# A chunked state recurrence: two heads in 64x64 products, or side by side in 128x128 products with block-diagonal operands

## The chip, the core and the metric

The kernel runs on one core of a Trainium2 chip, as one program. The metric is the device time of one execution in microseconds (us), the median of three runs. The engines are named as in the profile: PE is the matrix engine (TensorE; PEld is its weight load), DVE the vector engine, ACT the scalar engine, POOL GpSimd, and SP the engine that issues the DMAs.

## What is computed

One layer of a streaming encoder for 64 frames of a running stream and 512 of a new one (576 rows, width 1024): a norm, a combined projection, RWKV-7 time mixing, a gated mixer, a merge, a feed-forward part. The change is in time mixing. Each of 16 heads has a state S of 64x64 that goes from frame to frame:

```
def step(S, inp):
    r_t, w_t, k_t, v_t, a_t, b_t = inp
    sa = jnp.einsum('bhvk,bhk->bhv', S, a_t)
    S = S * w_t[:, :, None, :] + sa[..., None] * b_t[:, :, None, :] + v_t[..., None] * k_t[:, :, None, :]
    y = jnp.einsum('bhvk,bhk->bhv', S, r_t)
    return S, y
```

After it y is normalised by head, a bonus is added, and the sum is multiplied by a gate.

## The kernel before

The recurrence is not run frame by frame. The 576 frames are nine chunks of 64, the first of them the running stream's. In a chunk the removals (the a and b terms) depend on each other through a triangular 64x64 system, which is inverted; then the chunk needs only products with the state at its start. Heads go in eight pairs, head 0 of a pair on partitions 0 to 63 and head 1 on 64 to 127. The order is written for a pair as four generators, and each runs beside the generators of the neighbouring pairs.

- *Elements* (`elementwise`, lines 592 to 737): DVE, ACT and POOL make the rows AR, BK, AK and their factors from the projections r, k, v (tiles `pj`). PE makes the products `am` of one chunk's rows; DVE and POOL scale them into AB, AK and BK (lines 655 to 686). PE transposes BK (`tb`) and v (`tv`); ACT copies the results to BKt and Vt. The norms `n2` come from PE, `rn` is their reciprocal.
- *Inverse* (from line 739): AB goes out by DMA (`d_inv`) and comes back as M in 32x32 blocks. DVE runs 62 dependent operations in turns on Xt and X (lines 754 and 757). X goes out and back by DMA, DVE transposes (`T`, line 769), PE makes the two 32x32 products `mp` and `mu`, and ACT copies them to PT and AB.
- *Chain* (from line 793, printed below): nine chunks in eight steps, the first of which takes the running stream's chunk and the new one's first together. In a step the values product AK·Vt and the state product AR·S are summed in `pw`; ACT copies W; AB·W goes to `pz` and BKt·Vt to `pn`; ACT scales Z from `pz`; BKt·Z is added in `pn`; DVE makes the next S (line 825). Each product is two of 64x64, one head in the upper left and one in the lower right quarter of PE's array. `pw`, `pz` and `pn` are parts of one PSUM buffer `pc`, of which there is one. At the end of a pair the output rows `py` come from AR·S, AK·Vt and AB·Z over all chunks.
- *Finish* (from line 844): normalisation by DVE, ACT and POOL, nine transposes `to`, gate products `g`.

PE's order is written by `Weave`, a planner that keeps a clock of its own: a step that yields `LAT["W"]` is taken up again when its count of PE time has passed that latency, and between them it puts projection work three passes at a time (`pj`, later `gv`, each 128x128, in fp32r, as high and low parts in three products). The other engines are put in order by a scheduler, and each works strictly in its order; SP's DMA queue as well. ACT and POOL split the projection weights into `whi` and `wlo` in the same queues.

fp32 products take two passes of the array. Where the text below says a pair product, it means the two 64x64 products of two heads.

Of the kernel before, what the change touches and what calls it, by code (L numbers as in the profile page):

```python
# [12 lines left out]
P = 128  # L13
# [3 lines left out]
T = TS + TP  # L17
# [205 lines left out]
def layer(tc, I, O):  # L223
# [16 lines left out]
    cst = cp.tile([P, NCST], F32, name="cst")  # L240
# [4 lines left out]
    x0 = cst[0:3 * NU, C_X0:C_X0 + 11 * 32]  # L245
# [15 lines left out]
    def mmul(out, lhsT, rhs, **kw):  # L261
        n = 1
        for d in rhs.shape[1:]:
            n *= d
        clk.now += n * (1 if rhs.dtype == F32R else 4) / 2400
        return pe.matmul(out, lhsT, rhs, **kw)  # L266
# [205 lines left out]
    sp.dma_start(cst, I["cst"][:, 0:NCST])  # L472
# [18 lines left out]
    pool.memset(rmask[:, :, 0:1], 0.0)  # L491
    shc = cp.tile([P, 26, 2], F32, name="shc")
    s0 = cp.tile([P, NPAIR, HD], F32, name="s0")
    sp.dma_start(s0, I["s0"])
# [73 lines left out]
    rmul = ep.tile([P, NCH, P], F32, name="rmul")  # L568
    pool.tensor_copy(rmul[:, :, 64:P], mask[:, 64:P].unsqueeze(1).broadcast_to([P, NCH, 64]))
# [22 lines left out]
    def elementwise(E):  # L592
# [38 lines left out]
        s = ps1("n2")  # L631
        for c in range(NCH):
            p0 = 64 * (c % 2)
            mmul(s[p0:p0 + 64, c - c % 2:c - c % 2 + 2], q2[:, c * 64:(c + 1) * 64], bones[:, 0:P:64], start=True, stop=True)
        clk.now += LAT["n2t"]
        rn = rp.tile([P, NCH], F32, tag="rn", bufs=2, name="rn")
        for h in range(2):
            for par in range(2):
                dve.tensor_scalar(rn[64 * h:64 * h + 64, par::2], s[64 * par:64 * par + 64, h:10 - 2 * par:2], 1e-24, None, ALU.max)
        dve.reciprocal(rn, rn)  # L640
        pool.tensor_tensor(rmul[:, :, 0:64], mask[:, 0:64].unsqueeze(1).broadcast_to([P, NCH, 64]), rn.unsqueeze(2).broadcast_to([P, NCH, 64]), ALU.mult)
# [62 lines left out]
        Vt = rp.tile([P, NCH, HD], F32, tag="Vt", bufs=2, name="Vt")  # L704
        Z = rp.tile([P, NCH, HD], F32, tag="Z", bufs=2, name="Z")
        S = rp.tile([P, NCH + 2, HD], F32, tag="S", bufs=2, name="S")

        pvs = [ps1("tv").rearrange("p (j h v) -> p j h v", h=2, v=HD) for _ in range(2)]
        for j in range(5):
            t0 = min(j * P, T - P)  # L710
            mtrans(pvs[j // 4][:, j % 4].rearrange("p h v -> p (h v)"), v[:, t0:t0 + P], ident)
        for h, rows in enumerate(HR):
            for par in range(2):
                act.activation(Vt[rows, par:8:2, :], pvs[0][HR[par], :, h, :], ACT.Copy)
            act.activation(Vt[rows, 8, :], pvs[1][HR[1], 0, h, :], ACT.Copy)
        yield LAT["tv"]
        act.activation(S[:, 0, :], s0[:, hp_, :], ACT.Copy)
        pool.memset(S[:, 1, :], 0.0)
# [16 lines left out]
        E.update(AR=AR, AB=AB, AK=AK, BKt=BKt, Vt=Vt, Z=Z, S=S, eC=eC, rn=rn, bonus=bonus)  # L735
# [3 lines left out]
    def inverse(E):  # L739
        AB, di = E["AB"], d_inv[E["hp"]]  # L740
# [5 lines left out]
        X = rp.tile([n, 11, 32], F32, tag="X", name="X")  # L746
        pool.tensor_copy(X, x0.rearrange("p (i t) -> p i t", t=32))
# [10 lines left out]
        for g in range(3):  # L758
            r = (32 - g + 2) // 3
            sp.dma_start(di[1].rearrange("h c b s t -> (h c b) s t")[:, g:32:3, :], X[g * NU:(g + 1) * NU, 0:r, :])  # L760
        for h in range(2):
            for b in range(2):
                r0_ = 64 * h + 32 * b
                sp.dma_start(AB[r0_:r0_ + 32, :, 32 * b:32 * b + 32], di[1, h, :, b].rearrange("c s t -> s c t"))
        yield lat("U", E["hp"])
        T1 = rp.tile([P, NCH, 32], F32, tag="T1", name="T1")
        PT = rp.tile([P, NCH, 32], F32, tag="PT", name="PT")
        for h in range(2):
            dve.transpose(T1[64 * h:64 * h + 32], AB[64 * h:64 * h + 32, :, 0:32])
        yield lat("mp", E["hp"])  # L770
        pp = ps1("mp")
        for c in range(NCH):
            for h in range(2):
                a0, a1 = 64 * h, 64 * h + 32
                mmul(pp[a1:a1 + 32, c * 32:c * 32 + 32], AB[a0:a1, c, 32:64], T1[a0:a1, c, :], start=True, stop=True)
        for h in range(2):
            a1 = 64 * h + 32
            src = pp[a1:a1 + 32, 0:NCH * 32].rearrange("p (c t) -> p c t", t=32)
            act.activation(PT[a1:a1 + 32], src, ACT.Copy)
        yield lat("mu", E["hp"])  # L780
        pp = ps1("mu")
        for c in range(NCH):
            for h in range(2):
                a0, a1 = 64 * h, 64 * h + 32
                mmul(pp[a0:a1, c * 32:c * 32 + 32], PT[a1:a1 + 32, c, :], AB[a1:a1 + 32, c, 32:64], start=True, stop=True)
        for h in range(2):
            a0 = 64 * h
            src = pp[a0:a0 + 32, 0:NCH * 32].rearrange("p (c t) -> p c t", t=32)
            act.activation(AB[a0:a0 + 32, :, 32:64], src, ACT.Copy)
# [3 lines left out]
    def chain(E):  # L793
        AR, AB, AK, BKt, Vt, Z, S, eC, rn, hp_ = (E[n] for n in ("AR", "AB", "AK", "BKt", "Vt", "Z", "S", "eC", "rn", "hp"))
        Y = rp2.tile([P, NCH, HD], F32, tag="Y", bufs=2, name="Y")


        for cs in [(0, 1)] + [(c,) for c in range(2, NCH)]:
            n = len(cs)
            pw, pz, pn = ps1c("pc")[:, 0:384].rearrange("p (a i v) -> a p i v", a=3, v=64)  # L800
            first = lambda i: dict(start=i == 0, skip_group_check=True)
            for i, c in enumerate(cs):
                for rows in HR:
                    mmul(pw[rows, i], AK[rows, c, 0:64], Vt[rows, c, :], stop=False, **first(i))
            for i, c in enumerate(cs):
                for rows in HR:
                    mmul(pw[rows, i], AR[rows, c, 0:64], S[rows, c, :], start=False, stop=True, skip_group_check=True)
            W = rp.tile([P, 2, HD], F32, tag="W", bufs=2, name="W")
            act.activation(W[:, 0:n], pw[:, 0:n], ACT.Copy)  # L809
            yield LAT["W"]  # L810
            for i, c in enumerate(cs):
                for rows in HR:
                    mmul(pz[rows, i], AB[rows, c, 0:64], W[rows, i, :], stop=True, **first(i))
            for i, c in enumerate(cs):
                for rows in HR:
                    mmul(pn[rows, i], BKt[rows, c, 64:128], Vt[rows, c, :], start=False, stop=False, skip_group_check=True)
            for i, c in enumerate(cs):
                act.activation(Z[:, c, :], pz[:, i], ACT.Copy, scale=rn[:, c:c + 1])  # L818
            yield LAT["Z"]
            for i, c in enumerate(cs):  # L820
                for rows in HR:
                    mmul(pn[rows, i], BKt[rows, c, 0:64], Z[rows, c, :], start=False, stop=True, skip_group_check=True)
            for i, c in enumerate(cs):
                nxt = {0: NCH, NCH - 1: NCH + 1}.get(c, c + 1)
                dve.scalar_tensor_tensor(S[:, nxt, :], S[:, c, :], eC[:, c:c + 1], pn[:, i], ALU.mult, ALU.add)  # L825
                if nxt >= NCH:
                    sp.dma_start((O["wkv_s"] if c == 0 else O["wkv_p"])[hp_], S[:, nxt, :])
            if c < NCH - 1:
                yield LAT["S"]

        for c0, c1 in CV:
            py = ps1("py").rearrange("p (c t) -> p c t", t=64)
            for n, (w, w0, x) in enumerate(((AR, 64, S), (AK, 64, Vt), (AB, 64, Z))):
                for c in range(c0, c1):
                    for rows in HR:
                        mmul(py[rows, c - c0, :], w[rows, c, w0:w0 + 64], x[rows, c, :],
                             start=n == 0 and c == c0, stop=n == 2 and c == c1 - 1, skip_group_check=True)
            act.activation(Y[:, c0:c1, :], py[:, 0:c1 - c0], ACT.Copy)
            yield LAT["y"]
# [500 lines left out]
```

## Time and profile before

| | |
|---|---|
| median of 3 runs | 1281.55 us (1281.29 to 1284.96) |
| the profiled execution's own time | 1281.43 us |
| its span | 1279.6 us |
| granted clock of PE | 0.975 |
| time mixing in the profile | about 55 to 665 us, the next stage's products (`pb`) from 730 us |

In a row of the timeline stand the start in us, the duration (of all instructions of the row), the engine, the line, the operation, the tile written and the tiles read, the size of the array used, the shape, the count, and in brackets an idle time before it with what ended it. Matmuls overlap, so the price of one is the distance between the starts of neighbours, not its duration. A row of the waits gives who waited for whom, in all, how often and the longest. A row of the groups has the mean of one instruction in ns behind the busy time.

### The profile page before, as it was taken

Reading aid. Unit: us, or ns where it says so; the run is one execution under the profiler, and the core shown is the slowest. Engines: PE = TensorE matmul, PEld = TensorE weight load, DVE = VectorE, ACT = ScalarE, POOL = GpSimd, SP = SyncE. Lnnn points to the kernel's source line nnn. Section 1 sums busy time; section 2 is a strip of 40 time slices with the busy share of each in tenths; the row PEclk is TensorE's granted clock in tenths of the full one; section 3 lists DMA queues with packets and bytes.
Section 4 is the critical chain, followed back from the end, with each engine's and each line's share of the span. In section 5 each row is a group of like instructions: output and inputs, shape, how many; then the busy total and the mean of one; then the engine's idle time right before and its main releaser. Section 6 shows DMA issues by size and latency. Waiting matters only on the chain.

```text
span 1279.6 us, 26938 instructions
## 1 busy us (share of the span) xinstructions
PE 1209.6 (95%) x11306; PEld 1149.0 (90%) x11306; DVE 605.9 (47%) x1241; ACT 497.0 (39%) x976; POOL 615.6 (48%) x504
## 2 busy tenths in 40 slices
PE   7798999899989999999989999989999999999997
PEld 6798788889888988879889999989999999999997
DVE  5958656746575747464183533374333333310013
ACT  5644454545362645443351233453222222222220
POOL 6655243433534342442375645356655556544442
PEclk9899999899999999999999999989999999999998
DMA  5232222222221222323156543222222222242222
GB/s 194 72 103 85 69 80 71 87 60 89 69 94 58 78 84 75 88 81 105 52 180 198 157 151 109 84 108 82 83 83 83 84 85 85 83 160 79 87 74 75
DMA packets 72665, 122.35 MB, mean 96 GB/s; under 512 B 36032, under 2 KB 39360, under 8 KB 72544
## 3 DMA queue, kind: packets, MB, share of 16 engines
q1 hardware_dynamic: 72400, 120.56, 29.7%
q8 instruction: 89, 1.46, 0.5%
q14 instruction: 32, 0.26, 0.1%
q10 hardware_dynamic: 144, 0.07, 0.0%
HBM read 103.28 MB, written 17.33 MB: 94 GB/s over the span
## 4 chain that ended last, share of the span: by engine, by line
PE 72%; DVE 14%; DMA 4%; ACT 3%; issue 3%; POOL 2%; SPq 1%; DVEq 0%; ACTq 0%; POOLq 0%
PE fg L266 20%; PE po L266 14%; PE pj L266 13%; PE pb L266 4%; PE gv L266 4%; PE pc L266 4%; PE pa L266 3%; DVE Xt L754 3%; DVE X L757 3%; DMA M<-d_inv 2%; PE fp L266 1%; PE am L266 1%; PE z L266 1%; PE py L266 1%; POOL wlo L285 1%
## 5 line engine op out<-in xcount | busy, mean ns | idle before, releaser
L285 POOL TENSOR_TENSOR wlo<-raw,whi 128x512 fp32r<-128x512 f32 (+1 forms) x288 | 405.0, 1429 | 362.3 <-ACT whi L282 349.0
L282 ACT ACTIVATE whi<-raw 128x1024 fp32r<-128x1024 f32 x144 | 150.0, 1046 | 280.5 <-PE fg L266 172.5
L754 DVE TENSOR_TENSOR Xt<-X,M 108x84 f32<-108x84 f32 (+23 forms) x248 | 70.4, 284 | 34.2 <-DMA M<-d_inv 27.3
L757 DVE TENSOR_TENSOR X<-X,Xt 108x84 f32<-108x84 f32 (+23 forms) x248 | 70.6, 285 | 7.7
L1091 DVE TENSOR_TENSOR rs<-rs,nsq 128x288 f32<-128x288 f32 (+2 forms) x12 | 9.1, 756 | 105.5 <-ACT nsq L1090 105.5
L825 DVE SCALAR_TENSOR_TENSOR S<-S,eC,pc 128x64 f32<-128x64 f32 x72 | 19.3, 277 | 69.3 <-PE pc L266 61.5
L1159 DVE TENSOR_TENSOR ft<-ft,fg 128x288 f32<-128x288 f32 x40 | 16.4, 451 | 67.1 <-PE fg L266 65.5
L1153 DVE TENSOR_TENSOR fg<-fg,rs 128x288 f32<-128x288 f32 x40 | 16.5, 453 | 62.1 <-PE fg L266 62.0
L809 ACT ACTIVATE W<-pc 128x64 f32<-128x64 f32 (+1 forms) x64 | 14.7, 230 | 75.2 <-PE pc L266 74.6
L818 ACT ACTIVATE Z<-pc,rn 128x64 f32<-128x64 f32 x72 | 21.6, 312 | 46.8 <-PE pc L266 46.4
L1156 DVE SCALAR_TENSOR_TENSOR ft<-ft,fg 128x576 f32<-128x576 f32 (+1 forms) x24 | 28.6, 1192 | 19.0 <-ACT ft L1155 19.0
L627 POOL TENSOR_TENSOR aq<-aq,k 128x576 f32<-128x576 f32 x8 | 11.3, 1418 | 53.1 <-DVE k L458 51.8
L1157 POOL TENSOR_TENSOR ft<-ft,rs 128x576 f32<-128x576 f32 (+1 forms) x24 | 31.7, 1322 | 7.7 <-DVE ft L1156 7.7
L695 ACT ACTIVATE BKt<-tb 64x256 f32<-64x256 f32 (+1 forms) x96 | 31.2, 325 | 6.8 <-PE tb L270 5.3
L266 PE MATMUL pj<-h4l,whi 128*128 128x288 f32 x92 | 28.3, 308 | 5.5 <-DVE h4l L335 5.5
L266 PEld LDWEIGHTS pc<-Vt,AK 64*64 64x64 f32 x288 | 14.2, 137 | 21.2 <-DVE S L825 12.1
L266 PE MATMUL pc<-Vt,AK 64*64 64x64 f32 x288 | 22.6, 245 | 10.8 <-DVE S L825 10.6
L856 POOL TENSOR_TENSOR gm<-gm,mhalf 128x9 f32<-128x9 f32 x8 | 15.5, 1940 | 34.8 <-DVE gm L855 34.8
L266 PE MATMUL pj<-h5h,whi 128*128 128x288 f32 x92 | 31.1, 338 | 0.0
L266 PE MATMUL pj<-h4h,whi 128*128 128x288 f32 x92 | 30.9, 336 | 0.0
L266 PE MATMUL pj<-h3h,whi 128*128 128x288 f32 x92 | 30.5, 331 | 0.0
L266 PE MATMUL pj<-h6h,whi 128*128 128x288 f32 x92 | 29.8, 324 | 0.0
(1206 smaller groups left out, 4293.7 us busy)
## 6 DMA issues: line engine op xcount, KB each, us to landing
raw<-in_w_in SPq DMA_DIRECT2D x50, 512.0 KB
raw<-in_w_gate SPq DMA_DIRECT2D x22, 512.0 KB
raw<-in_w_up SPq DMA_DIRECT2D x22, 512.0 KB
raw<-in_w_down SPq DMA_DIRECT2D x16, 512.0 KB
raw<-in_w_gv SPq DMA_DIRECT2D x8, 512.0 KB
raw<-in_w_proj_a SPq DMA_DIRECT2D x8, 512.0 KB
raw<-in_w_proj_b SPq DMA_DIRECT2D x8, 512.0 KB
raw<-in_w_o SPq DMA_DIRECT2D x8, 512.0 KB
```

What stands on the lines that cost most here:

```text
L266: return pe.matmul(out, lhsT, rhs, **kw)
L282: keep(act.activation(hi[:, :cols], raw[:, :cols], ACT.Copy))
L285: keep(pool.tensor_tensor(lo[:, c0:c1], raw[:, c0:c1], f(hi[:, c0:c1]), ALU.subtract))
L695: act.activation(BKt[rows, c0:c1, part], pt[part, 0:c1 - c0, rows], ACT.Copy)
L754: ins = dve.tensor_tensor(t3, X[:, 0:r, s:s + 1].broadcast_to([n, r, w]), M[:, s:s + 1, s + 1:32].broadcast_to([n, r, w]), ALU.mult)
L757: dve.tensor_tensor(X[:, 0:r, s + 1:32], X[:, 0:r, s + 1:32], t3, ALU.add)
L818: act.activation(Z[:, c, :], pz[:, i], ACT.Copy, scale=rn[:, c:c + 1])
L825: dve.scalar_tensor_tensor(S[:, nxt, :], S[:, c, :], eC[:, c:c + 1], pn[:, i], ALU.mult, ALU.add)
L1153: keep(dve.tensor_tensor(g[:, HS[h]], pg, rs2[:, HS[h]], ALU.mult))
L1156: keep(dve.scalar_tensor_tensor(t[:, ts], t[:, ts], 1.0, g[:, ts], ALU.add, ALU.mult))
L1157: pool.tensor_tensor(t[:, ts], t[:, ts], rs2[:, ts], ALU.mult)
L1159: dve.tensor_tensor(t[:, HS[h]], t[:, HS[h]], pu, ALU.mult)
```

## The change

The chain's products use the full array. AK, AR, AB and BKt of two heads stand side by side as they are (64 rows that feed W and 64 that give output rows), and the moving side becomes block-diagonal: `VB` (values), `Sin` and `Sb` (state), `Wb` (W) have one head on rows and columns 0 to 63 and the other on 64 to 127, with zeros elsewhere that POOL writes once at the start. `ZV` holds Z of both heads above the values. A chunk has four products where there were five pair products: values AK·VB, state AR·Sb, removals AB·Wb, update BKt·ZV. The output rows come out of the first three on partitions 64 to 127, and the loop for `py` goes. For this the removal rows are multiplied out ahead (`g2`, 9 pair products a pair), `mu` has twice the products, and POOL subtracts the unit matrix (`eye`). ACT copies half of W and DVE the other; DVE makes ZV, ACT copies the output rows Y; S is updated by two DVE operations. Transposes `to` are five, not nine; the copies of `tb` and `tv` are fewer; VB and Sin are filled by DMAs, and X by a DMA instead of a POOL copy. In the planner, "y" goes from `LAT`, "S" is 1.1 instead of 0.945, "g2" is 1.5, and a full-array fp32 product counts as at least 128 columns wide.

```diff
-    "M": 5.011, "U": 27.0, "mp": 1.34, "mu": 1.593, "ch0": 1.796, "ch1": 21.42, "W": 0.789, "Z": 0.945, "y": 0.8, "S": 0.945, "gn1": 2.973, "gn2": 3.703, "to": 2.623, "to1": 0.41, "g": 1.513,
+    "M": 5.011, "U": 27.0, "mp": 1.34, "mu": 1.593, "ch0": 1.796, "ch1": 21.42, "W": 0.789, "Z": 0.945, "S": 1.1, "g2": 1.5, "gn1": 2.973, "gn2": 3.703, "to": 2.623, "to1": 0.41, "g": 1.513,
...
+    NWB = 2
+    fixed = lambda name, *shape: rp.tile([P, *shape], F32, name=name)
+    Sin = [fixed(f"Sin{i}", P) for i in range(2)]
+    Sb = [fixed(f"Sb{i}", P) for i in range(2)]
+    Wb = [fixed(f"Wb{i}", P) for i in range(NWB)]
+    VB = [fixed(f"VB{i}", NCH, P) for i in range(2)]
+    IV = fixed("IV", NCH, 64)
+    IT = fixed("IT", NCH, 64)
+    for t in (*VB, IV, *Sin, *Sb, *Wb):
+        pool.memset(t, 0.0)
...
-            for part in HR:
-                for rows in HR:
-                    act.activation(BKt[rows, c0:c1, part], pt[part, 0:c1 - c0, rows], ACT.Copy)
+            act.activation(BKt[:, c0:c1, :], pt[:, 0:c1 - c0], ACT.Copy)
...
+        for rows in HR:
+            sp.dma_start(vb[rows, :, rows], ZV[64:128, :, rows])
+            sp.dma_start(Sin[hp_ % 2][rows, rows], I["s0"][rows, hp_, :])
...
+        dve.transpose(IT.rearrange("p c t -> p (c t)"), IV.rearrange("p c t -> p (c t)"))
...
+        pool.tensor_tensor(AB[:, :, 0:64], IV, eye.unsqueeze(1).broadcast_to([P, NCH, 64]), ALU.subtract)
...
+                    mmul(pp[rows, c - c0, :], IT[rows, c, :], AB[rows, c, 64:128], start=True, stop=True)
+            act.activation(AB[:, c0:c1, 64:128], pp[:, 0:c1 - c0], ACT.Copy)
...
-        for cs in [(0, 1)] + [(c,) for c in range(2, NCH)]:
...
+        pc = ps1c("pc").rearrange("p (r v) -> p r v", v=P)
+        steps = [(0, 1)] + [(c,) for c in range(2, NCH)]
+        go = lambda i: dict(start=i == 0, skip_group_check=True)
+        def values(cs):
             for i, c in enumerate(cs):
+                mmul(pc[:, c % 2], AK[:, c, :], vb[:, c, :], stop=False, **go(i))
+        values(steps[0])
+        for n, cs in enumerate(steps):
+            for c in cs:
+                if c != 1:
+                    mmul(pc[:, c % 2], AR[:, c, :], Sin[hp_ % 2] if c == 0 else Sb[(c - 1) % 2], start=False, stop=False, skip_group_check=True)
...
+            for c in cs:
+                w = Wb[wcount[0] % NWB]
+                wcount[0] += 1
+                act.activation(w[HR[0], HR[0]], pc[HR[0], c % 2, HR[0]], ACT.Copy)
+                dve.tensor_copy(w[HR[1], HR[1]], pc[HR[0], c % 2, HR[1]])
+                ws.append(w)
             yield LAT["W"]
+            for c, w in zip(cs, ws):
+                mmul(pc[:, c % 2], AB[:, c, :], w, start=False, stop=True, skip_group_check=True)
+            for c in cs:
+                dve.tensor_tensor(ZV[HR[0], c, :].rearrange("p (h v) -> p h v", v=HD), pc[HR[0], c % 2, :].rearrange("p (h v) -> p h v", v=HD),
+                                  rnf[:, c, :].unsqueeze(2).broadcast_to([64, 2, HD]), ALU.mult)
+                act.activation(Y[HR[c % 2], c // 2, :], pc[HR[1], c % 2, :], ACT.Copy)
             yield LAT["Z"]
             for i, c in enumerate(cs):
+                mmul(pc[:, 2 + c % 2], BKt[:, c, :], ZV[:, c, :], stop=True, **go(i))
+            for c in cs:
...
+                        dve.scalar_tensor_tensor(dst, src[rows, rows], eC[rows, c:c + 1], pc[rows, 2 + c % 2, rows], ALU.mult, ALU.add)
...
+            if n + 1 < len(steps):
+                values(steps[n + 1])
                 yield LAT["S"]
-
-        for c0, c1 in CV:
-            py = ps1("py").rearrange("p (c t) -> p c t", t=64)
...
```

The orders, as they are built, with the semaphores that an instruction waits for in brackets (`DVE_49`, `Activation_49`, `Pool_49`, `PE_49` count what these engines have done). On PE, at the end of the eighth chunk of the first pair, before: `pc<-Z,BKt` is the last product of the chunk, `pc<-Vt,AK` the first of the next.

```order
L266 MATMUL pc<-Z,BKt 64x64
L266 MATMUL pj<-h3h,whi 128x288
L266 MATMUL pj<-h3l,whi 128x288
L266 MATMUL pj<-h3h,wlo 128x288
L266 MATMUL pj<-h4h,whi 128x288
L266 MATMUL pj<-h4l,whi 128x288
L266 MATMUL pj<-h4h,wlo 128x288 [waits Pool_49]
L266 MATMUL pj<-h4h,whi 128x288
L266 MATMUL pj<-h4l,whi 128x288
L266 MATMUL pj<-h4h,wlo 128x288
L266 MATMUL pc<-Vt,AK 64x64 [waits DVE_49]
L266 MATMUL pc<-Vt,AK 64x64
```

Nine passes of the projection lie between them, and the second waits for DVE. After, at the same place: `pc<-ZV,BKt` is the update and `pc<-VB,AK` the values product of the next chunk.

```order
L267 MATMUL pj<-h5l,whi 128x288
L267 MATMUL pj<-h5h,wlo 128x288
L267 MATMUL pc<-ZV,BKt 128x128 [waits Activation_49]
L267 MATMUL pc<-VB_555,AK 128x128 [waits DVE_49]
L267 MATMUL pj<-h6h,whi 128x288
L267 MATMUL pj<-h6l,whi 128x288
L267 MATMUL pj<-h6h,wlo 128x288
L267 MATMUL pj<-h6h,whi 128x288
```

The values product stands directly behind the update and waits for DVE; the passes of the projection follow behind it, and ahead of the state product.

On DVE, in the chain of the first pair and the inverse of the second (`X` and `Xt` are the inverse's operations), before, from inside one chunk over its update of S into the next:

```order
L757 TENSOR_TENSOR X<-X,Xt 108x3x23 [waits DVE_49]
L754 TENSOR_TENSOR Xt<-X,M 108x88 [waits DVE_49]
L757 TENSOR_TENSOR X<-X,Xt 108x4x22 [waits DVE_49]
L754 TENSOR_TENSOR Xt<-X,M 108x84 [waits DVE_49]
L757 TENSOR_TENSOR X<-X,Xt 108x4x21 [waits DVE_49]
L825 SCALAR_TENSOR_TENSOR S<-S,eC,pc 128x64 [waits PE_49,Activation_49]
L754 TENSOR_TENSOR Xt<-X,M 108x80 [waits DVE_49]
L757 TENSOR_TENSOR X<-X,Xt 108x4x20 [waits DVE_49]
L754 TENSOR_TENSOR Xt<-X,M 108x95 [waits DVE_49]
L757 TENSOR_TENSOR X<-X,Xt 108x5x19 [waits DVE_49]
```

One operation in a chunk waits for PE, with the inverse's operations around it. After, one chunk: the half of W, ZV, and the two halves of S.

```order
L840 COPY Wb_554<-pc 64x64 [waits Activation_49]
L770 TENSOR_TENSOR Xt<-X,M 108x54 [waits DVE_49]
L773 TENSOR_TENSOR X<-X,Xt 108x2x27 [waits DVE_49]
L770 TENSOR_TENSOR Xt<-X,M 108x52 [waits DVE_49]
L846 TENSOR_TENSOR ZV<-pc,rnf 64x128 [waits PE_49]
L773 TENSOR_TENSOR X<-X,Xt 108x2x26 [waits DVE_49]
L770 TENSOR_TENSOR Xt<-X,M 108x75 [waits DVE_49]
L773 TENSOR_TENSOR X<-X,Xt 108x3x25 [waits DVE_49]
L770 TENSOR_TENSOR Xt<-X,M 108x72 [waits DVE_49]
L862 SCALAR_TENSOR_TENSOR Sb_552<-Sb_551,eC,pc 64x64 [waits PE_49]
L862 SCALAR_TENSOR_TENSOR Sb_552<-Sb_551,eC,pc 64x64
L773 TENSOR_TENSOR X<-X,Xt 108x3x24 [waits DVE_49]
```

Four operations of the chain stand in a chunk now, three of them behind waits on other engines, and the inverse's operations are divided among the places between them.

More of the change, by code (lines that the diff above doesn't have):

```diff
@@ new lines, in inverse @@
+        for a0, a1 in blocks:
+            act.activation(AB[a0:a1, :, 32:64], pp[a0:a1, 0:NCH], ACT.Copy)
+        yield lat("g2", E["hp"])
+        for c0, c1 in CV:
+            pp = ps1("g2").rearrange("p (c t) -> p c t", t=64)
+            for c in range(c0, c1):
+                for rows in HR:
+                    mmul(pp[rows, c - c0, :], IT[rows, c, :], AB[rows, c, 64:128], start=True, stop=True)
+            act.activation(AB[:, c0:c1, 64:128], pp[:, 0:c1 - c0], ACT.Copy)
+            yield 0.0
```

179 lines of the change are left out of this document (77 added, 102 removed).

## The prediction

> **What bounds the kernel now.** I read the engines' busy time first, then the two stretches of the time-mix stage, then the waits of TensorE (PE), then single rows.
>
> ```profile
> PE 1209.6 (95%) x11306; PEld 1149.0 (90%) x11306; DVE 605.9 (47%) x1241; ACT 497.0 (39%) x976; POOL 615.6 (48%) x504
> ```
>
> PE is busy 95% of the span. By stretch (columns: length, then busy time of PE, PEld, DVE, ACT, POOL with counts, granted clock, DMA share, GB/s), the stage that the change touches, 55 to 730 us:
>
> ```profile
> 55.00:640.00 585.00, 547.27 (x6374) 493.44 (x6373) 344.30 (x857) 275.02 (x647) 237.09 (x213) 0.97 0.26 79
> 640.00:730.00 90.00, 84.83 (x669) 82.07 (x668) 51.24 (x81) 30.57 (x43) 57.55 (x42) 0.98 0.53 167
> ```
>
> PE works 547.27 + 84.83 = 632.1 of 675.0 us there, so its queue sets the pace: 43 us are idle, and everything that PE must wait for is added to the stage unless it was filled with projection work. The rest of the kernel (before 55 us and after 730 us) keeps its work. The waits of PE in the whole execution (us, times, longest):
>
> ```profile
> PE pc L266 <- DVE S L825: 10.6, 10, 2.1
> PE mp L266 <- DVE T L769: 9.7, 6, 2.9
> ...
> PE pc L266 <- ACT W L809: 2.9, 8, 0.5
> PE pc L266 <- ACT Z L818: 2.4, 5, 0.6
> ```
>
> The first row matters most. One case of it:
>
> ```profile
> 202.27 1.39 DVE L672 TENSOR_TENSOR AK<-am,cst 64x512 f32<-64x512 f32 x2
> ...
> 202.63 0.29 PE L266 MATMUL pj<-h4h,wlo 128*128 128x288 f32 x1
> ...
> 203.69 0.28 DVE L825 SCALAR_TENSOR_TENSOR S<-S,eC,pc 128x64 f32<-128x64 f32 x1
> ...
> 204.03 0.33 PE L266 MATMUL pc<-Vt,AK 64*64 64x64 f32 x4 [1.10 <-DVE S L825]
> ```
>
> The values product (AK·Vt) at 204.03 does not read S, yet it starts 0.06 us after S has ended (203.69 + 0.28). The five products of a chunk share the one buffer `pc` (`bufs=1`): the next chunk's first product waits until DVE has read the state update from it. In the kernel before nine projection passes lie between the state product and the next values product, and the wait shows only when DVE is late (here two AK operations, 1.39 us). The Trainium skill, "PSUM — Partial Sum Buffer", section "PSUM bank collisions raise a hardware error", says that software must keep engines apart by bank and quadrant, not by address. The row agrees.
>
> **The change, part by part.** The profiled execution took 1281.43 us (span 1279.6, so 1.8 outside it), the median of the three runs is 1281.55; sums are made against 1281.43.
>
> *PE work.* A stretch of 64x64 products between projections:
>
> ```profile
> 570.46 0.29 PE L266 MATMUL pj<-h7h,wlo 128*128 128x288 f32 x1
> 570.68 0.33 PE L266 MATMUL pc<-W,AB 64*64 64x64 f32 x4
> 570.85 0.28 PE L266 MATMUL pc<-Vt,BKt 64*64 64x64 f32 x4
> 571.06 0.40 PE L266 MATMUL pj<-h7h,whi 128*128 128x288 f32 x1
> 571.30 0.29 PE L266 MATMUL pj<-h7l,whi 128*128 128x288 f32 x1
> ```
>
> Output rows, five pair products (20 records) at a time, with the neighbours that I use below:
>
> ```profile
> 572.03 0.28 PE L266 MATMUL gv<-whi,h1l 128*64 128x256 f32 x1
> ...
> 572.14 0.28 PE L266 MATMUL gv<-wlo,h1h 128*64 128x256 f32 x1
> ...
> 572.35 0.33 PE L266 MATMUL pc<-Z,BKt 64*64 64x64 f32 x4
> ...
> 572.52 0.75 PE L266 MATMUL py<-S,AR 64*64 64x64 f32 x20
> 572.80 0.28 DVE L825 SCALAR_TENSOR_TENSOR S<-S,eC,pc 128x64 f32<-128x64 f32 x1 [0.73 <-PE pc L266]
> 573.00 0.25 DVE L754 TENSOR_TENSOR Xt<-X,M 108x90 f32<-108x90 f32 x1
> ...
> 573.10 0.75 PE L266 MATMUL py<-Vt,AK 64*64 64x64 f32 x20
> ...
> 573.68 0.75 PE L266 MATMUL py<-Z,AB 64*64 64x64 f32 x20
> ```
>
> And six full-array fp32 passes between projections:
>
> ```profile
> 856.83 0.29 PE L266 MATMUL fp<-f1h,wlo 128*128 128x288 f32 x1
> 856.96 0.83 PE L266 MATMUL rb<-cst,rr 128*128 128x128 f32 x6
> 857.54 0.38 PE L266 MATMUL fp<-f2h,whi 128*128 128x288 f32 x1
> 857.76 0.30 PE L266 MATMUL fp<-f2l,whi 128*128 128x288 f32 x1
> ```
>
> A pair product costs (573.68 − 572.52)/10 = 0.117 us. A projection pass takes 0.13 (856.83 to 856.96). From 570.46 to 571.30 pass 0.84 us: two projections 0.26, two pair products 0.234, and 0.34 left, the price of changing the array's shape in and out. From 856.83 to 857.76 pass 0.93: two projections 0.26 and six full fp32 passes, 0.11 each, with nothing left over. So a full fp32 product (two passes) costs 0.223 us.
>
> Before, a head pair has seven steps of five pair products in three stretches (1.6 us each, 11.2), a first step of two chunks (10 × 0.117 + 3 × 0.34 = 2.2) and 27 output products, 3.2, with one stretch of their own, 0.3: 16.9, and 135 for eight pairs. After, 35 full products per pair, 7.8, and 62 for eight: −73. Given back: the removal rows g2, 72 pair products, 8.4, and some twelve stretches, 4; the second half of mu, 0 to 4, taken at 2; some twenty groups of am that lay against the chain's small products and shared their stretch, 7; transposes, 32 fewer of about 0.11, −3.5; n2 about +1. Sum **−54**; with 0.30 to 0.38 a stretch, −47 to −61.
>
> *The wait for S.* In the new order the values product stands directly behind the state product, and the yield that filled this place comes after it (the order in the part on the change). By the row at 204.03 it waits for the update of S. All of that is now PE idle time: 0.28 from the start of what follows the state product to S (572.52 to 572.80), 0.20 to the second half of S (572.80 to 573.00, the next independent operation), 0.28 for that half, 0.06 to PE: 0.82. Each half has as many elements per partition as the S of before, so I give it the same time. There are seven such places in each of eight pairs; one of the seven has four S operations, +0.40. 49 × 0.82 + 7 × 1.22 = **+49**. Ends: 0.65 if the halves overlap more (38) and 1.0 with the longer full-array pass (58). If only data, and not the buffer, made the product wait, this term would be 0, the lateness below would stay as it was before, and PE would again wait for the inverse: −54 + 10 + 2 with the later terms, 1239 us.
>
> *DVE late for S.* An operation of the inverse takes its place on DVE for 0.27:
>
> ```profile
> 159.53 0.24 DVE L754 TENSOR_TENSOR Xt<-X,M 108x80 f32<-108x80 f32 x1
> 159.80 0.24 DVE L757 TENSOR_TENSOR X<-X,Xt 108x80 f32<-108x80 f32 x1
> ```
>
> In about 24 steps four to six of them stand between ZV and the update of S, 1.1 to 1.6 us, while ZV, the Y copy, the state product and its hand-off need about 1.15: 0.2 late, 24 × 0.2 = 5. Long operations (AR, BK, AK, the transpose of the inverse) stood in the way ten times before, 10.6 us, after a cover of 9 × 0.13 − 0.62 = 0.55; the cover is gone, so ten times 1.06 + 0.55 = 16. Together **+21** (10 to 30), and the **−10.6** of before go.
>
> *W and Z.* The three forms on ACT that count:
>
> ```profile
> L282 ACT ACTIVATE whi<-raw 128x1024 fp32r<-128x1024 f32 x137 | 144.1, 1056 | 256.5 <-PE fg L266 167.9 <-PE po L266 45.2 <-PE pa L266 9.8
> ...
> L818 ACT ACTIVATE Z<-pc,rn 128x64 f32<-128x64 f32 x72 | 21.6, 312 | 46.8 <-PE pc L266 46.4
> ...
> L809 ACT ACTIVATE W<-pc 128x64 f32<-128x64 f32 x56 | 12.5, 223 | 65.1 <-PE pc L266 64.5
> ```
>
> W was one copy of 0.22, Z one of 0.31, with hand-offs 0.54 and 0.64 behind 1.17 us of nine projection passes. Now W is a half on ACT, then a half on DVE that waits for it, 0.28 + 0.22 + 0.06 + 0.23 + 0.06 = 0.85; Z is ZV on DVE, then the Y copy on ACT, and the state product waits for Y, 0.9 to 0.95. The slack falls from about 0.6 to 0.3, and to 0.1 where the nine passes are gv passes of 0.11 (572.03, 572.14), while a whi split that is in the way on ACT holds 1.06. Thirteen waits, 5.3 us, become some thirty of 0.4; the first step's chunks go through in turn, 8 × 0.4. **+10** (3 to 18).
>
> *The inverse.* It runs beside the chain, from am to mp:
>
> ```profile
> 343.08 0.39 PE L266 MATMUL am<-AR,BK 64*64 64x128 f32 x6
> ```
>
> and
>
> ```profile
> 383.11 0.22 PE L266 MATMUL mp<-T,AB 32*32 32x32 f32 x2 [2.13 <-DVE T L769]
> ```
>
> That is 40 us, of which the inverse's 62 operations on DVE (first and last) take 25:
>
> ```profile
> 352.79 0.19 DVE L754 TENSOR_TENSOR Xt<-X,M 108x31 f32<-108x31 f32 x1 [1.90 <-DMA M<-d_inv]
> ...
> 377.59 0.18 DVE L757 TENSOR_TENSOR X<-X,Xt 108x11 f32<-108x11 f32 x1
> ```
>
> Counted in PE's order at the prices above, PE had 36 to 38 us of work there in most pairs, hence the mp waits and, after the long ones, half clock (0.50, the third column from the right):
>
> ```profile
> 247.00:260.60 13.60, 12.20 (x134) 11.01 (x134) 6.54 (x13) 2.42 (x6) 8.05 (x5) 0.50 0.18 63
> ...
> 383.50:390.20 6.70, 6.19 (x86) 5.78 (x86) 0.46 (x1) 0.81 (x2) 0.23 (x1) 0.50 0.38 126
> ```
>
> With the S waits, PE's way from am to mp becomes 41 to 45 us in all but the first pair. mp waits fall from 9.7 to about 2, and of the 6.8 + 3.3 us lost at half clock half goes: **−13** (−20 to 0). *Smaller:* g2 has 15 projection passes, 2.0 us, behind ACT's copies in most pairs and less in two; nine memsets on POOL stand ahead of the first pair's aq and ta; VB's and Sin's DMAs, on SP behind the value copies, have a whole chain of the pair before as cover: **+2** (0 to 8).
>
> Sum: −54 + 49 + 21 − 10.6 + 10 − 13 + 2 = +4: **1285 us**.
>
> **The rivals.** *Slower, 1303: the inverse becomes the pace.* DVE now waits four times a step (W, ZV, S and what feeds them) instead of once, in order, with the inverse's 62 operations between. If their run grows from 25 us to over 28 (the point from which 40 passes PE's 43), mp waits and half clock stay (+13) and S is late by 0.4 rather than 0.2 (+5). For it: 17 inverse operations stand in a step now, 12 before, with 344 us of DVE work in 585 already. Against: a step of 5.9 us holds 17 × 0.27 = 4.6.
>
> *Faster, 1264: the idle time of PE serves DVE.* The S wait gives DVE 0.8 us more a step, so long operations are finished earlier: lateness 5 instead of 21, and all half clock goes (−5). For it: DVE is busy only 59% of the stretch. Against: the places of AK and BK ahead of S are fixed in DVE's order.
>
> *No wait for S, 1239* (worked out above): against it stand all ten waits of the first row. *The 0.34 stays, 1350:* it would belong to the hand-off between engines and not to the array's shape, so that each of 64 steps keeps three of them, 64 × 3 × 0.34 = 65. Against it: the stretch at 570.68 waits for nothing that is late and pays it.
>
> **How the numbers follow.** A measurement can tell about 0.3%, 3.8 us, from no change. The forecast's case 0.46, its own range 1275 to 1295 (0.07 faster, 0.17 same, 0.22 slower); the slower rival 0.25; the faster 0.24; no wait 0.02; the 0.34 stays 0.03. Faster 0.33, same 0.17, slower 0.50. The range 1260 to 1307 takes in the first three and leaves out the last two and the tails.
>
> **What would show it.** PE work of the stage falls by about 50 us and its idle time grows by as much. Right: a row of PE's waits, pc from DVE's S, with about 56 cases and 50 to 75 us, each values product 0.05 to 0.06 us behind an S; small products only in am, mp, mu, g2. Wrong: that row under 30 us (then the time is near 1240), or chain steps that cost over 0.34 beside full-array products, or mp waits over 9.7 us (the slower rival), or S mostly on time with less than 0.9 us a case (the faster one).

## The result and the profile after

The changed kernel takes 1373.62 us (median of 4 runs, 1369.83 to 1376.57), the kernel before 1283.13 (median of 4): a ratio of 1.0704, 95% interval 1.067 to 1.0737. That is 90 us slower, where 1285 was predicted and 1307 was the upper end.

```profile
PE 1211.7 (88%) x10042; PEld 1161.9 (85%) x10042; DVE 659.3 (48%) x1457; ACT 464.6 (34%) x864; POOL 638.2 (47%) x514
```

PE was busy 95% of 1279.6 us before and is busy 88% of 1372.2 now. The first product of the stage behind time mixing (`pb`) starts at 824.0 us, against 730.0: 94.0 us later, so all of the span's loss, 92.6 us, lies ahead of it, in time mixing. In three stretches (columns as in the prediction):

```profile
55.00:650.00 595.00, 484.84 (x4513) 447.12 (x4511) 367.09 (x958) 221.55 (x482) 237.83 (x202) 0.92 0.26 74
650.00:752.00 102.00, 84.68 (x785) 79.32 (x785) 53.83 (x148) 35.92 (x76) 37.40 (x30) 1.00 0.29 87
752.00:824.00 72.00, 65.93 (x476) 63.62 (x477) 31.93 (x49) 16.38 (x21) 42.07 (x30) 0.95 0.55 166
```

In the first one PE is busy 484.84 of 595 us (547.27 of 585 before), and the granted clock is 0.92 (0.97 before). The waits of PE:

```profile
PE pc L267 <- DVE Sb L862: 47.0, 48, 2.4
PE pc L267 <- ACT Y L848: 15.6, 22, 3.5
PE pc L267 <- DVE Wb L840: 15.5, 19, 2.8
PE pc L267 <- DVE Sb L859: 14.1, 8, 3.2
...
PE mp L267 <- DVE IT L784: 6.3, 2, 4.5
...
PE am L267 <- DVE AR L676: 4.9, 1, 4.9
```

The four rows of `pc` shown here hold 92.2 us; the three of before held 15.9. S has 48 + 8 = 56 cases, the number in the prediction. One of them, PE and DVE:

```profile
401.77 0.39 PE L267 MATMUL pc<-ZV,BKt 128*128 128x128 f32 x2
...
402.20 0.59 DVE L862 SCALAR_TENSOR_TENSOR Sb<-Sb,eC,pc 64x64 f32<-64x64 f32 x2 [1.18 <-PE pc L267]
...
402.84 0.49 PE L267 MATMUL pc<-VB,AK 128*128 128x128 f32 x2 [0.68 <-DVE Sb L862]
...
403.08 0.38 PE L267 MATMUL pj<-h5h,whi 128*128 128x288 f32 x1
...
403.30 0.29 PE L267 MATMUL pj<-h5l,whi 128*128 128x288 f32 x1
```

The two passes of the update start at 401.77 and 401.88. DVE's two halves of S follow from 402.20 to 402.79, and the values product starts 0.05 us later. From the last pass to the product pass 0.96 us, of which 0.11 is the pass itself: 0.85, against 0.82 worked out ahead (where the prediction says "state product" in front of a wait for S, it means this update product). The 0.68 in brackets is less, because a busy PE is counted to the modelled end of a matmul; sums over starts are larger than the rows of waits. A product that was not waited for, in the same chain:

```profile
410.43 0.29 PE L267 MATMUL pj<-h1h,wlo 128*128 128x288 f32 x1
410.56 0.38 PE L267 MATMUL pc<-Sb,AR 128*128 128x128 f32 x2
410.70 0.38 PE L267 MATMUL pj<-h2h,whi 128*128 128x288 f32 x1
410.93 0.29 PE L267 MATMUL pj<-h2l,whi 128*128 128x288 f32 x1
```

From 410.43 to 410.93 pass 0.50 us: two projection passes, 0.26, and 0.24 for the full product. After a wait it takes more: from 402.84 to 403.30 pass 0.46, a projection pass of 0.13 and 0.33.

### The profile page after: what moved, and what is told of

It is laid out like the page before. It is cut to its first block, busy times and chain, and to the rows that moved or that the text cites. A ratio compares the mean times of both kernels' runs of the same rounds, so it can differ in the third digit from the quotient of the medians.

```text
span 1372.2 us, 24583 instructions
## 1 busy us (share of the span) xinstructions
PE 1211.7 (88%) x10042; PEld 1161.9 (85%) x10042; DVE 659.3 (48%) x1457; ACT 464.6 (34%) x864; POOL 638.2 (47%) x514
## 4 chain that ended last, share of the span: by engine, by line
PE 45%; DVE 4%; issue 3%; POOL 1%; ACT 1%; DMA 1%; POOLq 0%; DVEq 0%; ACTq 0%
PE fg L267 18%; PE po L267 13%; PE pb L267 4%; PE pa L267 3%; PE gv L267 2%; PE pc L267 1%; POOL wlo L286 1%; PE z L267 1%; PE pj L267 1%; DVE y L1155 1%; DMA wsT<-in_wsT 1%; PE fp L267 0%; DVE Sb L862 0%; DVE y L1152 0%; DVE bst L1003 0%
## 5 line engine op out<-in xcount | busy, mean ns | idle before, releaser
L267 PE MATMUL pc<-VB,AK 128*128 128x128 f32 x144 | 34.5, 333 | 61.1 <-DVE Sb L862 47.0
L267 PEld LDWEIGHTS pc<-VB,AK 128*128 128x128 f32 x144 | 22.4, 201 | 72.5 <-DVE Sb L862 56.1
L840 DVE COPY Wb<-pc 64x64 f32<-64x64 f32 x72 | 15.6, 216 | 76.7 <-ACT Wb L839 75.6
L267 PE MATMUL pc<-Wb,AB 128*128 128x128 f32 x144 | 30.6, 303 | 18.3 <-DVE Wb L840 15.5
L704 POOL TENSOR_TENSOR BK<-BK,EL 128x512 f32<-128x512 f32 (+1 forms) x24 | 20.0, 831 | 56.7 <-PE am L267 56.6
L267 PE MATMUL pc<-ZV,BKt 128*128 128x128 f32 x144 | 31.1, 308 | 16.1 <-ACT Y L848 15.6
L267 PEld LDWEIGHTS pc<-Wb,AB 128*128 128x128 f32 x144 | 21.2, 189 | 26.5 <-DVE Wb L840 19.2
L848 ACT ACTIVATE Y<-pc 64x128 f32<-64x128 f32 x72 | 19.6, 273 | 69.3 <-DVE ZV L846 68.7
L267 PEld LDWEIGHTS pc<-ZV,BKt 128*128 128x128 f32 x144 | 22.1, 196 | 23.6 <-ACT Y L848 22.6
L887 POOL TENSOR_TENSOR gm<-gm,mhalf 128x10 f32<-128x10 f32 x8 | 16.2, 2027 | 41.6 <-DVE gm L886 41.6
L862 DVE SCALAR_TENSOR_TENSOR Sb<-Sb,eC,pc 64x64 f32<-64x64 f32 x96 | 26.6, 278 | 17.6 <-PE pc L267 16.1
```

The lines of the kernel that those rows point to most:

```text
L704: pool.tensor_tensor(BK[:, c0:c1], BK[:, c0:c1], EL[:, c0:c1, 64:65].broadcast_to([P, c1 - c0, P]), ALU.mult)
L848: act.activation(Y[HR[c % 2], c // 2, :], pc[HR[1], c % 2, :], ACT.Copy)
L862: dve.scalar_tensor_tensor(dst, src[rows, rows], eC[rows, c:c + 1], pc[rows, 2 + c % 2, rows], ALU.mult, ALU.add)
```

## The experiments

A hand-off is what another engine does between two products of the chain on PE; its cover is the projection work that PE has to do meanwhile. The theory was that the hand-offs in the one buffer, above all the uncovered wait for S, are the loss; the rivals were DVE's queue as the pace, and products that cost more than was worked out.

### The cover put back (e1_cover)

```diff
             if n + 1 < len(steps):
-                values(steps[n + 1])
                 yield LAT["S"]
+                values(steps[n + 1])
```

> The changed kernel with one line moved: the planner's yield for S stands ahead of the next values product instead of behind it, so that nine or more projection passes lie between the state update product and the product that waits for the update of S. Theory (the wait for S, uncovered in 56 places, is the largest cost): of the 71 us that PE loses behind the state product some 15 to 20 stay, where DVE is late by more than the cover; half-clock time falls by 5 to 10 us, waits for the inverse come back by some 5: 1310 to 1325 us. Rival (DVE's queue is the pace, and a cover on PE only moves the wait to the next product): 1350 or more, with the waits at W, ZV or the inverse up by what S loses.

1303.11 us, 1.0164 of before (1.013 to 1.0198): 70 us of the 90 are gone with one line moved. The waits of PE:

```profile
PE pc L267 <- DVE Wb L840: 25.1, 29, 2.9
PE pc L267 <- ACT Y L848: 10.8, 16, 1.4
PE mp L267 <- DVE IT L784: 10.8, 3, 5.8
...
PE pc L267 <- DVE Sb L862: 4.0, 6, 1.0
```

The wait for S falls from 61.1 us to 4.0, and 1.8 in the row of L859, more than the theory allowed, since the cover of nine or more passes also takes up DVE's lateness. The waits at W rise from 15.5 to 25.1, those for the inverse from 6.3 to 10.8: a part of the rival is true, but a small one.

### The update in a buffer of its own (e2_bank)

```diff
+            pn = ps1("pn").rearrange("p (r v) -> p r v", v=P)
-                mmul(pc[:, 2 + c % 2], BKt[:, c, :], ZV[:, c, :], stop=True, **go(i))
+                mmul(pn[:, c % 2], BKt[:, c, :], ZV[:, c, :], stop=True, **go(i))
```

(S is read from `pn`; the order is that of the changed kernel.)

> The changed kernel with the state update product written to another PSUM buffer than the other three (one of the three that the helpers share). Order as in the changed kernel. Theory (one shared buffer ties the products together): the values product no longer waits for S, the state product no longer waits for the copy of Y; the waits ahead of the values products fall from 71 to under 15 us, those ahead of the state products from 21 to about 10, AR·S waits for a late DVE some 10, half clock down by 10: 1290 to 1305 us. Rival (DVE's queue is the pace): AR·S waits instead, 1340 or more. Second rival (the buffer taken from the helpers is missed): S is on time, but tb, tv, mu and g2 wait for buffers, over 1320.

1296.04 us, 1.0101 (1.0067 to 1.0135).

```profile
PE pc L267 <- DVE Wb L840: 27.0, 30, 2.9
...
PE pn L267 <- DVE ZV L846: 7.4, 10, 1.0
...
PE pc L267 <- ACT Y L848: 2.6, 6, 1.0
```

The order of PE is unchanged, and still the values product does not wait for S any more. So it was the buffer, and not the data, that tied them. The update waits for ZV (7.4) instead of for the copy of Y behind it (15.6).

### The kernel before with the cover taken away (e3_before_uncovered)

```diff
+            if cs[0]:
+                yield LAT["S"]
             for i, c in enumerate(cs):
                 for rows in HR:
                     mmul(pw[rows, i], AR[rows, c, 0:64], S[rows, c, :], start=False, stop=True, skip_group_check=True)
...
-            if c < NCH - 1:
-                yield LAT["S"]
```

> The kernel before with only the cover taken away: the yield for S stands behind the next values product AK·Vt and ahead of AR·S, so AK·Vt follows BKt·Z at once and waits for S. Number of small-product stretches unchanged. Theory: 56 waits of about 0.55 us plus DVE's lateness that the cover hid, 35 to 50 us, and some half clock: 1318 to 1340 us. Rival (the loss comes from the full-array products, their copies or the planner, not from this place): within 8 us of the kernel before.

1323.71 us, 1.032 (1.029 to 1.035): 41 us of loss in the kernel before, with its small products and single copies.

```profile
PE pc L266 <- DVE S L827: 41.6, 56, 2.8
PE pc L266 <- ACT W L811: 6.9, 18, 0.9
```

56 waits, 41.6 us. The place alone makes these 41 us, without any full-array product. The changed kernel loses more behind its update, 61.1 us by its rows: there S takes two DVE operations, here one. How the rest divides was not tried.

### No hand-offs at all, after and before (e4_after_no_handoff, e7_before_no_handoff)

In the changed kernel the copies of W and Y, the ZV product and the updates of S are left out, in the kernel before the copies of W and Z and the updates of S; the products read constant tiles. Every product of PE stays.

```diff
-                act.activation(w[HR[0], HR[0]], pc[HR[0], c % 2, HR[0]], ACT.Copy)
-                dve.tensor_copy(w[HR[1], HR[1]], pc[HR[0], c % 2, HR[1]])
...
-                        dve.scalar_tensor_tensor(dst, src[rows, rows], eC[rows, c:c + 1], pc[rows, 2 + c % 2, rows], ALU.mult, ALU.add)
```

> The changed kernel without the chain's hand-offs: no copies of W, no ZV product, no copy of Y, no update of S; the chain's products read constant tiles (the chain's arithmetic is left out, every product on PE stays). It shows PE's own work. Theory (full-array products are cheaper on PE by 50 us than the stretches before, all of the loss is waiting): 1205 to 1230 us. Rival (the full-array products cost PE more than was worked out): over 1260.

> The kernel before without the chain's hand-offs: no copies of W and Z, no update of S; the chain's products read constant tiles (the chain's arithmetic is left out, every product on PE stays). To be set beside the changed kernel without hand-offs, 1257 us, where PE waits 14 us at am, 12.5 at z and 9 at n2 for the elementwise work of the next pair. Theory (PE's own work is 45 to 50 us less after the change, but half of it goes to those waits): 1260 to 1275 us, with those waits under 12 us together and PE's small-product stretches as in the kernel before. Rival (the full-array products are not cheaper): 1250 or less.

One run each: 1257.12 us after, 1259.65 before. The first expectation fails: the changed kernel without any hand-off was to take 1205 to 1230, and its rival asked for over 1260. Its waits, the three largest in time mixing:

```profile
PE am L267 <- DVE AR L676: 11.5, 4, 4.7
PE z L267 <- DVE bonus L748: 11.4, 7, 2.9
PE n L267 <- ACT q L636: 8.3, 3, 4.0
```

And the kernel before without hand-offs:

```profile
PE mp L266 <- DVE T L769: 9.7, 6, 3.3
...
PE z L266 <- DVE bonus L733: 3.4, 5, 2.0
...
PE n L266 <- ACT q L623: 2.8, 1, 2.8
PE am L266 <- DVE AR L658: 2.6, 1, 2.6
```

Where PE was to gain, it waits for the rows of the next pairs: 31.2 us for AR, the bonus and the squares of k, against 8.8 for the same three. From 55 us to the first `pb`, PE is busy for 598.0 us after and 629.2 before, 31 less, and idle for 53.9 and 25.3, 29 more. It also spends 65 us at half clock there instead of 34, which costs it 18 us instead of 11. So, clock for clock, PE is busy for some 38 us less, and with nothing to wait for in its chain the changed kernel gains 2.5 us on the one before, which single runs can't tell from nothing: the saving goes to waits for element work on DVE and ACT (22 of the 29 us are those three rows) and to half clock (7 us). The kernel before came out 0.35 us below the range expected for it, with those waits under 12 us as expected.

### W on ACT, with and without the tied buffer (e5_bank_w_act, e12_w_on_act_alone)

```diff
-                dve.tensor_copy(w[HR[1], HR[1]], pc[HR[0], c % 2, HR[1]])
+                act.activation(w[HR[1], HR[1]], pc[HR[0], c % 2, HR[1]], ACT.Copy)
```

> The kernel with the update in its own buffer, and both halves of W copied by ACT instead of one by ACT and one by DVE. In the run with the update in its own buffer, PE waits 27 us for the DVE half of W, the largest row. Theory (the half on DVE stands behind the inverse and long operations in DVE's queue, after it has waited for ACT): the row falls by 10 to 18 us, 1278 to 1288 us. Rival (ACT's queue, with weight splits of 1.05 us, makes W late, and the DVE half only comes last): the row stays over 22 us under ACT's name, 1292 to 1300.

> The changed kernel with one part undone: both halves of W copied by ACT, everything else as changed, the one buffer and the uncovered S too. Theory (the half on DVE stands behind DVE's queue and costs about half of the 23 us of W waits): 1355 to 1366 us. Rival (only the order around S counts, since time saved at W is waited for at S): within 5 us of the changed kernel.

With the update in its own buffer the edit is worth 15 us: 1281.4 us, 0.9981 (0.9965 to 0.9997), from 1296.04.

```profile
PE pn L267 <- DVE ZV L846: 14.9, 18, 2.5
...
PE pc L267 <- ACT Wb L840: 5.2, 9, 1.5
```

PE's wait for W falls from 27.0 to 5.2, and the wait for ZV rises from 7.4 to 14.9, though DVE, which makes ZV, has one copy less. In the changed kernel as it is, the same edit is worth 5: 1368.35 us, 1.0653 (1.0637 to 1.0669).

```profile
PE pc L267 <- DVE Sb L862: 43.9, 48, 2.7
PE pc L267 <- ACT Y L848: 26.2, 30, 3.6
PE pc L267 <- DVE Sb L859: 13.9, 8, 3.2
...
PE pc L267 <- ACT Wb L840: 5.2, 5, 2.7
```

W falls from 15.5 to 5.2 there, too, but Y rises from 15.6 to 26.2: most of the time saved at one hand-off is waited for at the next. (ACT, which makes Y, has one copy more here; how much of the 26.2 that makes was not tried.) The theory's 8 to 18 us are missed; the rival (within 5 us) describes it at its edge.

### More cover for W (e6_bank_w_act_cover)

```diff
-    "W": 0.789, "Z": 0.945, "S": 1.1,
+    "W": 1.15, "Z": 0.945, "S": 1.1,
```

> As the one before, with the planner's latency for W raised from 0.789 to 1.15, so that about twelve projection passes instead of nine stand between the state product and the removals product. Theory (what is left of the W waits is lateness of 0.3 to 0.9 us beyond the cover): W waits fall under 8 us, 1265 to 1278 us, below the kernel before. Rival (the passes are missed later: the chain of a pair ends later, and the elementwise work or the inverse of the next pairs is what PE waits for): within 5 us of the one before.

1278.17 us, 0.9943 (0.9924 to 0.9962): 0.6% below the kernel before, with an interval that leaves out 1, and 0.2 us above the theory's range. The W waits are under 8 us, as the theory asked, but the gain on e5 is 3.2 us, which the rival (within 5) foresaw.

```profile
PE pn L267 <- DVE ZV L846: 15.3, 15, 1.7
...
PE pc L267 <- ACT Wb L840: 2.9, 4, 1.3
```

### More cover for Z, and ZV on ACT (e10_cover_w_and_z, e11_zv_on_act)

```diff
-    "W": 1.15, "Z": 0.945, "S": 1.1,
+    "W": 1.15, "Z": 1.1, "S": 1.1,
```

> The version with the update in its own buffer, W on ACT and W's latency at 1.15 in the planner, with Z's raised from 0.945 to 1.1 as well. PE waits 15 us for ZV there, 15 times. Theory (a longer cover hides lateness): the ZV row falls to about 5, 1268 to 1276 us. Rival (the passes are missed at the end of the chain or by the elementwise work, PE waits elsewhere): 1276 to 1282.

1282.37 us, 0.9986 (0.9969 to 1.0003). The row for ZV falls to 11.2 us and the time does not fall: the waits at mp, am and W are each some 2 us longer than in e6 (6.5, 4.4 and 4.8 us after 4.6, 2.0 and 2.9). That is what the rival said; the time is 0.4 us above its range.

```diff
-                dve.tensor_tensor(ZV[HR[0], c, :].rearrange("p (h v) -> p h v", v=HD), pc[HR[0], c % 2, :].rearrange("p (h v) -> p h v", v=HD),
-                                  rnf[:, c, :].unsqueeze(2).broadcast_to([64, 2, HD]), ALU.mult)
+                for h, cols in enumerate(HR):
+                    act.activation(ZV[HR[0], c, cols], pc[HR[0], c % 2, cols], ACT.Copy, scale=rnf[:, c, h:h + 1])
```

(on e6, without the cover for Z)

> The version with the update in its own buffer, W on ACT and W's latency at 1.15, with ZV made by two operations on ACT instead of one on DVE, so that DVE has only the update of S in the chain. Theory (a hand-off through DVE is late because of its long queue): the ZV row falls from 15 to under 8 us, 1268 to 1276. Rival (ACT, which has W, Y and the weight splits, becomes the late one): the row stays or grows under ACT's name, 1278 to 1290.

1276.41 us, 0.994 (0.9921 to 0.9959): the lowest median of the versions that leave no arithmetic out, and not to be told from e6.

```profile
PE pn L267 <- ACT ZV L847: 11.2, 11, 3.4
PE pc L267 <- DVE Sb L863: 9.1, 7, 2.1
```

ZV falls from 15.3 to 11.2, S comes back with 9.1 after 1.9. Neither side of the expectation is clear.

### Without the inverse's operations (e8_after_no_inverse_ops, e9_after_no_inverse_ops_again)

60 of the 62 operations of each inverse are left out of the changed kernel, so the inverse isn't computed.

```diff
-            for s in range(0, 31):
+            for s in range(0, 1):
```

> The changed kernel with 60 of the 62 DVE operations of each inverse left out (the inverse isn't computed; everything else stays). Theory (the wait for S is mostly the bare hand-off of 0.95 us from the last state pass to the next product, and DVE's queue adds a third): the waits behind the state product fall from 71 us to 55, those at W and ZV from 44 to 25, half clock to 15: 1325 to 1340 us. Rival (DVE's queue is the cause and the hand-off alone is hidden): under 1300.

> The changed kernel with 60 of the 62 DVE operations of each inverse left out (the inverse isn't computed; everything else stays), run again because PE ran at less than a third of its speed in the first run, from the start. Theory (the wait for S is mostly the bare hand-off of 0.95 us, and DVE's queue adds a third): waits behind the state product fall from 71 us to about 55, those at W and ZV from 44 to 25, half clock falls: 1320 to 1340 us. Rival (DVE's queue is the cause): under 1300.

The first run took 3973.73 us and says nothing of the edit, which only takes work off DVE: its projection passes come every 0.43 us from the first on, long before the inverse.

```profile
22.31 0.75 PE L267 MATMUL pfg<-u1h,wlo 128*128 128x288 f32 x1
22.74 0.75 PE L267 MATMUL pfw<-u2h,whi 128*128 128x288 f32 x1
```

The second took 1351.09 us (2 runs), 1.0519 (1.0489 to 1.0548), 22 less than the changed kernel.

```profile
PE pc L267 <- DVE Sb L862: 39.3, 48, 2.4
PE pc L267 <- ACT Y L848: 15.4, 21, 2.2
PE pc L267 <- DVE Sb L859: 14.9, 8, 3.2
PE pc L267 <- DVE Wb L840: 13.6, 19, 2.5
```

The waits for S fall from 61.1 to 54.2 us, and those at W and Y hardly move (29.0 after 31.1). The waits at mp are gone (6.3 us in the changed kernel). It comes out slower than both sides expected. From 55 us to the first `pb` DVE is busy for 335 us instead of 453, and the wait for S stays: most of it is the bare hand-off, at least 0.83 us at each of the 56 places, 46 us. And the lateness at W and Y, which I had set against the inverse's operations, comes mostly from other work: in this run's trace DVE's half of W stands behind AK (about 1 us), the running sums `L` (1.14), `q` (1.8) and `bonus` (0.46), or ACT's half behind weight splits `whi` (1.05).

## Why the prediction was wrong

- *What bounds the kernel, and the tied buffer.* Right. e2 and e3 show it: the values product waits for S through the buffer, in either kernel, and it costs far more where the cover is missing (10.6 us with it and 41.6 without, in the kernel before).
- *The wait for S, +49 and +21 for late DVE.* Right in size. Over the 56 places the values product starts 1.37 us after the last update pass on average (0.94 at least, 3.47 at most); less the pass of 0.11 that is 70.6 us, against 70. The parts fit, too: at the shortest it is 0.83 us at 48 places and 1.37 at the eight with four operations, 51 us in all against 49, and the lateness beyond that is 20 against 21. The share of the inverse's operations in it was small in the forecast, 5, and small in e9, 7.
- *W and Z, +10.* This step failed. Counted by starts, PE loses 23.5 us ahead of the removals products and 20.8 ahead of the updates, 44 in place of 15. The bare hand-offs were right (W 0.78 us, forecast 0.85; Y 0.90, forecast 0.9 to 0.95); the lateness was not. I took the thirteen waits of before and made them thirty of 0.4; by starts PE waits at 56 of the 128 places, 0.8 us on average. A hand-off that passes ACT and then DVE is late when either queue is, and a lateness of 1 to 3 us, rare in each queue, isn't bounded by a cover of 0.3:

```profile
313.69 2.54 POOL L286 TENSOR_TENSOR wlo<-raw,whi 128x512 fp32r<-128x512 f32 x2 [5.31 <-ACT whi L283]
...
315.13 1.22 DVE L770 TENSOR_TENSOR Xt<-X,M 108x90 f32<-108x90 f32 x1
315.18 0.38 PE L267 MATMUL pc<-Sb,AR 128*128 128x128 f32 x2
...
315.65 0.22 ACT L839 ACTIVATE Wb<-pc 64x64 f32<-64x64 f32 x1 [2.03 <-PE pc L267]
...
317.52 0.46 DVE L748 TENSOR_TENSOR bonus<-bo,v 128x288 f32<-128x288 f32 x1
...
318.18 0.22 DVE L840 COPY Wb<-pc 64x64 f32<-64x64 f32 x1
...
318.45 0.49 PE L267 MATMUL pc<-Wb,AB 128*128 128x128 f32 x2 [1.96 <-DVE Wb L840]
```

The state product starts at 315.18, ACT's half of W is there at 315.87, and DVE comes to its half at 318.18, behind six operations of the inverse and the bonus, the first of which takes 1.22 us: 1.96 us of waiting in one place. In other places it is AK, `L` or `q` that DVE has in hand, and e9, without the inverse's operations, loses as much at W by starts, 23.4 us. e5 shows that DVE's half was the dear one.
- *The inverse, −13.* This step failed in sign. The waits at mp fell only from 9.7 to 6.3 us, and half clock did not go but grew. I expected it only behind the long waits at mp. Now the hand-offs bring it about, too, singly or added up (the third column from the right is the granted clock):

```profile
546.50:549.90 3.40, 1.44 (x21) 1.03 (x24) 1.53 (x5) 0.27 (x1) 0.00 (x0) 1.00 0.00 0
549.95:553.30 3.35, 3.35 (x34) 3.02 (x27) 2.17 (x4) 0.22 (x1) 1.05 (x1) 0.50 0.03 5
```

In the first of these pieces PE is busy for 1.44 of 3.4 us, with one wait for Y and one for S; in the next it has half its clock. Of the twenty falls in time mixing eleven follow hand-offs of the chain: four of them two shorter waits like these, seven a single one of 1.9 to 3.3 us. Before, it was one of seven. Half clock holds 102 us there instead of 38, and pass by pass PE loses 24 us to it instead of 11. That the waits cause it is argued from the times (with the cover back, e1, the loss is 14), not tried by itself; and they are not all of it, since e4, with no hand-off in the chain, still loses 18 us.
- *PE's work, −54.* The prices were right: 0.22 to 0.24 for a full product that isn't waited for, and 0.34 for a stretch (the middle one of 81 stretches of the chain before in which nothing waits). Stretches of small products fell from 213 to 54 in time mixing, −54 us; more products take some 5 back, and the 112 products that wait for S, W, ZV or Y, 0.1 dearer each, some 11, which was not foreseen: about −38. In e4 beside e7, where none waits for a hand-off, it is −46 by starts.
- *Smaller, +2.* About ten in all: the wait for AR at am is 4.9 instead of 3.7, and gate products, transposes and `pa` wait for copies and splits.

By these terms: W and Z some 29 over, half clock and mp 23, PE's work 16, the rest 8 to 10, of the 88 us between forecast and result; about ten are not assigned.

- *The rivals.* The slower one (1303) had the right sign and the wrong mechanism: the inverse was not the pace, since leaving its operations out gains 22 of 90 us, and the waits at mp fell. The faster one asked for a lateness that falls with the waits; it did not. The one without a wait for S falls with its 56 cases, "the 0.34 stays" with the row at 410.56.

Beside the sizes, the terms were added as if they were independent. With the waits as large as this, time gained at one comes back in part at the next (e5, e12), and the time that PE saves is not time that the kernel saves (e4 beside e7).

## What to carry to other kernels

Where several products of a dependent chain share one buffer, look for what stands between a read of it by another engine and the next write: independent work has to be issued there, ahead of the write, and work that is issued behind it hides nothing. A hand-off through two engines in turn is late when either queue is, so its cover must be set against the long operations in both queues, not against the hand-off's own times. And when PE's work is made shorter, run both versions once without their hand-offs: here that tells that the saving of some 38 us on PE leaves 2.5 us or nothing in the time.

## What the runs showed of the hardware

- The granted clock changes on a grid of 3.41 us. In time mixing, in the profiles before and after, each of the 23 pieces of the grid in which PE was idle for over 1.9 us was followed by a piece at half clock, whether the idle time was one wait or several. With 1.7 to 1.9 us idle some were and some were not; with less the clock fell twice. (The piece from 546.50 above has 1.96 us.) The Trainium skill, "TensorE: Matmul & The Clock Gate", section "Why this matters for your kernels", asks for no idle gap of over some 3 us. Here the sum of shorter gaps in a piece sufficed, and the measurement decides.
- A full product that was waited for takes 0.33 us (counted as above, from starts), 0.327 to 0.335 at 48 places outside half clock in the profile after. One that was not waited for takes 0.22 to 0.24 at most places.
- One operation of the inverse on DVE took 1.22 us instead of 0.25 (315.13 above), while POOL was at a weight split (the row at 313.69). In the profile after, 30 of the 496 operations of the inverse took over 0.5 us, and each ran beside an operation on POOL, most often such a split; of the other 466, 433 ran beside none. Before it was 32 of 496, again each beside one (573.57, 1.23 us). That POOL's work is the cause was not tried.
- In one run (e8) PE went at less than a third of its speed, 0.43 us a projection pass where 0.13 is usual, with a granted clock of 1.00 in the records; the same kernel took 1351 us the next time, on another chip.
